# Transposing the meta queries' probabilities from full tiles of 128 rows

## The chip, the cores and the metric

One core of a Trainium2 chip runs the whole network in one launch. The metric is device time in microseconds (us); the kernel before is given by the median of three runs, and one further execution was profiled.

## The reference

A four-layer encoder works on 272 tokens (16 learned meta tokens and 256 grid tokens) of 2048 features in float32. Each layer projects its input into queries, keys, values and a gate, attends, multiplies by the SiLU of the gate, projects back, adds the residual times a constant and normalises:

```python
proj = h @ w_in                       # q, k, v, z
y    = attention(q, k, v) * silu(z)   # by layer: A, B, C, A
h    = layer_norm(ALPHA * h + y @ w_out[i])
```

Layer kind A is attention in a window of the grid plus the meta keys, 16 heads; here the 16 meta queries attend to the 16 meta keys alone. Kind B is differential attention, 8 heads of two softmaxes each, a = p1 - lambda * p2, over all 272 keys; here the meta queries attend to all keys without bias. Kind C is a sliding window with a sink in the softmax, 16 heads that share 4 key heads; here the meta queries again attend to the meta keys alone. In the last layer the meta tokens are no longer needed as queries.

## The kernel before

Everything lies with features on the partitions and tokens on the free axis, in the order: 128 grid tokens, 16 meta tokens, 128 grid tokens. A projection of 128 output features is 16 contraction steps of three matmuls each (`mm3`, lines 146 to 150: high times high, high times low, low times high, in a float32 form of 12 significant bits), each with 128x128 weights and 272 moving columns. The weights stream in from HBM, and ScalarE (line 156) and VectorE (line 157) split them into the high and low part.

Around this one long stream of weight matmuls on TensorE (`run`, lines 817 to 878) the rest is done by background tasks, Python generators that are advanced one step for each four contraction steps (`step`, line 183). The attention of a head is such a task: `attn_a`, `attn_b` or `attn_c`. A planner that simulates the timeline then sets the order of the instructions on each engine, from the dependencies and the order in which they were written; so a task's TensorE instructions stand between weight matmuls in the places that the planner gives them. At the borders between layers the norm of the one layer has to be finished on VectorE, ScalarE and GpSimd before the weight matmuls of the next can go on.

In each attention the probabilities P of 128 + 128 grid queries (tile `s`) and 16 meta queries (tile `s2`, 16 partitions) lie with queries on the partitions. For P times V they are transposed by TensorE into one PSUM tile `tr`. A transposition is a float32 matmul whose stationary operand is the data, loaded as weights, and whose moving operand is the identity matrix `ident`: as many columns move as the data has rows.

- Layer A, `attn_a`: lines 453 and 460 transpose four 96-key pieces of the grid queries, line 455 the meta queries: stationary 16 rows x 96 columns, moving 16 columns. Line 463 transposes the values. The tile `s2` is zeroed on GpSimd for each head (line 413), since only columns 32 to 47 are written.
- Layer B, `attn_b`: lines 528, 529 and 530 run twice per head, for the keys 0 to 127 and 144 to 271; line 529 is that of the meta queries (stationary 16x128, moving 16). Lines 534 to 536 transpose the keys 128 to 159, laid side by side three times by `thrice` (line 364, a GpSimd copy at line 372); line 535 is that of the meta queries (16x96, moving 16). Lines 544 and 545 transpose the values.
- Layer C, `attn_c`: line 648 transposes the grid queries, lines 649 to 651 the three-fold keys; line 650 is that of the meta queries (16x96, moving 16). Before it GpSimd zeroes `s2_mid` for each head (line 370) and copies into it (line 372).

So in layers A, B and C there are 16, 8 x 2 + 8 and 16 transpositions with 16 rows, 56 in all; the last layer has none. The setup (line 231 on) makes `ident`, the constants and the input operands; GpSimd's queue there also issues small loads, such as `lnp` (line 261), the norms' parameters, which ScalarE splits along with the first weights.

Of the kernel before, what the change touches and what calls it, by code (L numbers as in the profile page):

```python
# [11 lines left out]
F32 = mybir.dt.float32  # L12
# [8 lines left out]
META = 16  # L21
NTOK = SEQ + META
# [5 lines left out]
ALPHA = (2 * DEPTH) ** 0.25  # L28
# [3 lines left out]
CHUNK = 4  # L32
LOOKAHEAD = 8
WARM = 8
DEFERRED = 7  # column tiles of a layer that multiply u, while its statistics and its input are made
TAIL = (8, 10, 11)  # first k of the last norm whose subtraction and product GpSimd does, and whose affine VectorE
SETS = (("hh", "hl"), ("yh", "yl"))
BUFS = {"raw": 3, "wh": LOOKAHEAD + 1, "wl": LOOKAHEAD + 1, "qh": 2, "ql": 2, "kh": 2, "kl": 2,
        "vs": 2, "ez": 1, "gate": 3, "bias": 2, "s": 3, "s2": 2, "nm": 4, "sm": 4, "nm2": 4, "sm2": 4,
# [4 lines left out]
# Token order on chip: grid columns 0..31 (row index fastest), the meta tokens,  # L44
# grid columns 32..63.  Tiles keep it as [2, 144]; the last 16 columns are unused.
# [8 lines left out]
def in_tiles(kind):  # L54
    """Column tiles of an input projection in the order of their use: (key, tile)."""
    t = []
    if kind == "A":
        for h in range(16):
            t += [(("q", h), h), (("k", h), 16 + h), (("v", h), 32 + h), (("z", h), 48 + h)]
    elif kind == "B":  # L60
        for h in range(8):
            t += [(("q", 2 * h), 2 * h), (("k", 2 * h), 16 + 2 * h),
                  (("q", 2 * h + 1), 2 * h + 1), (("k", 2 * h + 1), 16 + 2 * h + 1),
                  (("v", 2 * h), 32 + 2 * h), (("v", 2 * h + 1), 32 + 2 * h + 1),
                  (("z", 2 * h), 48 + 2 * h), (("z", 2 * h + 1), 48 + 2 * h + 1)]
    else:
        for g in range(4):
            h = 4 * g
            t += [(("k", g), 16 + g), (("v", g), 20 + g)]
            order = [("q", h), ("q", h + 1), ("z", h), ("q", h + 2), ("z", h + 1),  # L70
                     ("q", h + 3), ("z", h + 2), ("z", h + 3)]
            t += [((n, i), i if n == "q" else 24 + i) for n, i in order]
    return t


def granules(layer):
    """(matrix, column tile, first k, key) in the order in which TensorE takes them."""
    out = []
    t = in_tiles(KINDS[layer])
    if layer == 0:  # L80
        for k0 in range(0, KT, GRAN):
            out += [("in", e, k0, key) for key, e in t[:3]]
        t = t[3:]
    else:
        for key, e in t[:2]:
            out += [("in", e, k0, key) for k0 in range(0, KT - GRAN, GRAN)]
        out += [("in", e, KT - GRAN, key) for key, e in t[:2]]
        t = t[2:]
    for key, e in t:
        out += [("in", e, k0, key) for k0 in range(0, KT, GRAN)]  # L90
    for m in range(3):
        out += [("out", m, k0, ("o", m)) for k0 in range(0, KT - GRAN, GRAN)]
    out += [("out", m, KT - GRAN, ("o", m)) for m in range(3)]
    for m in range(3, KT):
        out += [("out", m, k0, ("o", m)) for k0 in range(0, KT, GRAN)]
    return out
# [18 lines left out]
class Emit:  # L115
# [36 lines left out]
    def hilo(self, src, hi, lo, scale=None):  # L152
        """hi + lo == scale * src, hi with 12 significant bits."""
        nc = self.nc
        if scale is None:
            nc.scalar.copy(out=hi, in_=src)  # L156
            nc.vector.tensor_sub(out=lo, in0=src, in1=hi.bitcast(F32))  # L157
        else:
            nc.scalar.activation(hi, src, AF.Copy, scale=scale)
            nc.vector.scalar_tensor_tensor(out=lo, in0=src, scalar=scale, in1=hi.bitcast(F32),  # L160
                                           op0=ALU.mult, op1=ALU.subtract)

    def column_sums(self, src, view):
        """The sums over the 128 features, on every partition."""
        nc = self.nc
        h, l = self.tok(F32R, "sumh"), self.tok(F32R, "suml")
        self.hilo(view(src), view(h), view(l))
        yield
        p = self.ptok("sc")
        nc.tensor.matmul(view(p), lhsT=self.ones_r, rhs=view(h), start=True, stop=False)  # L170
        nc.tensor.matmul(view(p), lhsT=self.ones_r, rhs=view(l), start=False, stop=True)
        return p

# [57 lines left out]
    def setup(self, nlayers):  # L231
        nc = self.nc
# [9 lines left out]
        x = [self.tok(F32, f"yh{k}") for k in range(KT)]  # L242
# [16 lines left out]
        nc.gpsimd.memset(self.zero, 0.0)  # L259
        self.lnp = self.st([128, DEPTH, KT, 2], F32, "lnp")  # L260
# [14 lines left out]
    def lam_task(self):  # L275
        """-lambda of the differential attention on every partition."""
# [17 lines left out]
    def rows(self, key, acc, view, l, scale=None):  # L294
        """(x, b) with the projection of the layer's input = x + b, and each times scale.

        The first tiles of a layer but the first multiply u = g * d, g and b of the norm before them:
        W' h = (W' u - mean * W' g) * rstd + W' b.  The other tiles multiply h itself."""
# [34 lines left out]
    def evac_gate(self, key, acc, view, l):  # L333
        """z * sigmoid(z)"""
# [11 lines left out]
    def finish(self, k, y, view):  # L346
        """y of 128 features into the operands of the output projection."""
# [8 lines left out]
    def stack(self, src, tag, low):  # L356
        """Rows 0..95 of src hold one block three times: hi, but lo in the 32 rows from low."""
# [5 lines left out]

    def thrice(self, tag, src):
        """src [p, ..., n <= 32] as [p, ..., 3, 32], the rest 0."""
# [38 lines left out]
    def attn_a(self, h, last):  # L404
        """Window attention: query tile 0 sees the key columns 0..191, tile 1 the columns 96..271."""
# [5 lines left out]
        if not last:  # L411
            s2 = self.st([META, 96], F32, "s2")
            nc.gpsimd.memset(s2, 0.0)
# [17 lines left out]
        if not last:  # L431
            p2, nm2, sm2 = s2[:, 32:48], self.st([META, 1], F32, "nm2"), self.st([META, 1], F32, "sm2")
# [14 lines left out]
        # The chunks of P: 0 of tile 0, then 1 of tile 0, the meta queries and 0 of tile 1, for the keys 96..191  # L447
        # that these share, then 1 of tile 1.
# [3 lines left out]
        for c in range(3):  # L452
            nc.tensor.transpose(tr[:96, at[c]:at[c] + 128], s[:, c // 2, c % 2 * 96:c % 2 * 96 + 96], ident)  # L453
        if not last:
            nc.tensor.transpose(tr[:96, 256:272], s2, ident[:META, :META])
# [26 lines left out]
    def attn_b(self, h):  # L482
# [5 lines left out]
        for j in range(2):  # L488
# [3 lines left out]
            s2 = self.st([META, NTOK], F32, "s2")  # L492
# [19 lines left out]
            e.append((s, s2))  # L512
            sums.append((sm, sm2))
# [10 lines left out]
        s_mid, s2_mid = self.thrice("s_mid", s[:, :, mid]), self.thrice("s2_mid", s2[:, mid])  # L524
        ph, pl = self.st([128, 2, NTOK], F32R, "ph"), self.st([128, 2, NTOK], F32R, "pl")
        for c, ks in enumerate(keys):
            tr = self.pt("tr")
            nc.tensor.transpose(tr[:, 0:128], s[:, 0, ks], ident)
            nc.tensor.transpose(tr[:, 128:144], s2[:, ks], ident[:META, :META])
# [5 lines left out]
        nc.tensor.transpose(tr[:96, 128:144], s2_mid, ident[:META, :META])  # L535
# [43 lines left out]
    def rsqrt(self, src, scale, view=None):  # L579
        """(src * scale + 1e-5) ** -0.5 with one Newton step."""  # L580
# [23 lines left out]
    def attn_c(self, h):  # L604
# [5 lines left out]
        s2 = self.st([META, META + 1], F32, "s2")  # L610
# [33 lines left out]
        s_mid, s2_mid = self.thrice("s_mid", s[:, :, 128:160]), self.thrice("s2_mid", s2[:, :META])  # L644
# [5 lines left out]
        nc.tensor.transpose(tr2[:96, 128:144], s2_mid, ident[:META, :META])  # L650
# [21 lines left out]
    def residual(self, l, m, view):  # L672
        """ALPHA * h of 128 features, less the pivot where that is known in time."""
# [12 lines left out]
    def on_out(self, l, m, acc, view, last):  # L686
        """d = residual sum less a pivot (the mean of the first 512 features); its sums, and g * d as operands."""
# [55 lines left out]
    def norm_stats(self, l, view, last):  # L743
        """-mean of d, and the reciprocal of the deviation, of each token on every partition."""
# [29 lines left out]
    def normalise(self, l):  # L774
        """The input of layer l itself, from u."""
# [41 lines left out]
    def run(self, nlayers):  # L817
# [4 lines left out]
        for l in range(nlayers):  # L822
# [12 lines left out]
            if l:  # L835
                self.tasks.append(self.normalise(l))
            for which, e, k0, key in granules(l):
# [48 lines left out]
def weight_chunks(mats, nlayers):  # L886
    """The granules of all matrices, in the order of their use, CHUNK to a row of 8 KB per partition."""
# [8 lines left out]
def window_bias(rpb):  # L896
    """rpb laid out per head as [query, keys of tile 0, keys of tile 1]; 0 at the meta keys, -1e30 outside."""
# [58 lines left out]
```

## Time and profile before

| | |
|---|---|
| median of three runs | 2023.39 us (2023.30 to 2023.46) |
| span of the profiled execution, the only time that it gives | 2021.7 us, 1.7 below that median |
| TensorE, matmuls | 1975.4 us busy, 98% |
| TensorE, weight loads (beside the matmuls) | 1957.0 us, 97% |
| VectorE | 1456.9 us, 72% |
| ScalarE | 1107.3 us, 55% |
| GpSimd | 676.2 us, 33% |
| HBM | 159 GB/s over the span |

The share of the span says which engine is occupied, but a matmul's recorded duration runs on while the next has begun, so that what a matmul costs is read from the distance of its start to the next one's start, which is called its pitch below. Idle time of an engine that is not the bottleneck costs nothing.

### The profile page before, as it was taken

Reading aid. Unit: us, or ns where it says so; the run is one execution under the profiler, and the core shown is the slowest. Engines: PE = TensorE matmul, PEld = TensorE weight load, DVE = VectorE, ACT = ScalarE, POOL = GpSimd, SP = SyncE. Lnnn points to the kernel's source line nnn. Section 1 sums busy time; section 2 is a strip of 40 time slices with the busy share of each in tenths; the row PEclk is TensorE's granted clock in tenths of the full one; section 3 lists DMA queues with packets and bytes.
Section 4 is the critical chain, followed back from the end, with each engine's and each line's share of the span. In section 5 each row is a group of like instructions: output and inputs, shape, how many; then the busy total and the mean of one; then the engine's idle time right before and its main releaser. Section 6 shows DMA issues by size and latency. Waiting matters only on the chain.

```text
span 2021.7 us, 40776 instructions
## 1 busy us (share of the span) xinstructions
PE 1975.4 (98%) x15794; PEld 1957.0 (97%) x15794; DVE 1456.9 (72%) x2617; ACT 1107.3 (55%) x2396; POOL 676.2 (33%) x975
## 2 busy tenths in 40 slices
PE   9999999999989999999999899999998999999995
PEld 9999999999989999999999899999998999999995
DVE  7666666667998677777779986766898666666665
ACT  6555555455655555555556555655555555555553
POOL 2110011118683122212396832323965111111075
PEclk9999999999999999999999999999999999999998
DMA  8444444444534444444445244344444444554442
GB/s 289 156 160 169 160 169 160 165 152 162 189 125 147 148 166 147 159 160 148 148 165 188 105 156 158 139 157 158 161 171 149 166 169 170 175 174 162 162 166 84
DMA packets 52466, 324.00 MB, mean 160 GB/s; under 512 B 5904, under 2 KB 12064, under 8 KB 14768
## 3 DMA queue, kind: packets, MB, share of 16 engines
q1 hardware_dynamic: 51984, 320.76, 44.9%
q8 instruction: 124, 2.03, 0.4%
q0 software_dynamic: 288, 0.63, 0.1%
q14 instruction: 70, 0.57, 0.1%
HBM read 319.27 MB, written 2.10 MB: 159 GB/s over the span
## 4 chain that ended last, share of the span: by engine, by line
PE 92%; DVE 5%; issue 1%; POOL 1%; DMA 0%; ACT 0%; SPq 0%; DVEq 0%; POOLq 0%
PE acc L150 28%; PE acc L148 28%; PE acc L149 28%; DVE wl L157 2%; PE sc L150 1%; PE sc L149 1%; PE sc L148 1%; PE o L150 1%; PE o L149 1%; DVE ht L783 1%; PE o L148 1%; PE tr L453 1%; PE tr L463 1%; DVE yl L788 0%; DVE hl L788 0%
## 5 line engine op out<-in xcount | busy, mean ns | idle before, releaser
L157 DVE TENSOR_TENSOR wl<-raw,wh 128x512 fp32r<-128x512 f32 x1184 | 904.5, 770 | 458.7 <-ACT wh L156 446.5
L156 ACT CAST wh<-raw 128x512 fp32r<-128x512 f32 x1184 | 723.1, 618 | 629.7 <-PE acc L149 602.9
L150 PE MATMUL acc<-yh,wl 128*128 128x272 f32 (+2 forms) x2448 | 708.7, 289 | 0.0
L148 PE MATMUL acc<-yh,wh 128*128 128x272 f32 (+2 forms) x2448 | 706.3, 289 | 0.0
L149 PE MATMUL acc<-yl,wh 128*128 128x272 f32 (+2 forms) x2448 | 703.2, 287 | 0.0
L148 PE MATMUL acc<-hh,wh 128*128 128x272 f32 (+3 forms) x2288 | 660.9, 289 | 6.4 <-ACT wh L156 6.4
L149 PE MATMUL acc<-hl,wh 128*128 128x272 f32 (+3 forms) x2288 | 663.6, 290 | 0.0
L150 PE MATMUL acc<-hh,wl 128*128 128x272 f32 (+3 forms) x2288 | 661.6, 289 | 0.2 <-DVE wl L157 0.2
L149 PEld LDWEIGHTS acc<-yl,wh 128*128 128x128 f32 x2448 | 463.0, 189 | 0.1
L148 PEld LDWEIGHTS acc<-yh,wh 128*128 128x128 f32 x2448 | 461.9, 189 | 0.3
L150 PEld LDWEIGHTS acc<-yh,wl 128*128 128x128 f32 x2448 | 462.0, 189 | 0.0
L148 PEld LDWEIGHTS acc<-hh,wh 128*128 128x128 f32 x2288 | 433.1, 189 | 7.3 <-ACT wh L156 7.1
L150 PEld LDWEIGHTS acc<-hh,wl 128*128 128x128 f32 x2288 | 433.2, 189 | 0.8 <-DVE wl L157 0.7
L149 PEld LDWEIGHTS acc<-hl,wh 128*128 128x128 f32 x2288 | 432.9, 189 | 0.5
L342 DVE RECIPROCAL ez<-ez 128x272 f32<-128x272 f32 (+1 forms) x64 | 116.7, 1824 | 22.7 <-POOL ez L340 22.7
L410 POOL MEMSET s<- 128x16 f32 x32 | 3.6, 112 | 354.2 <-PE tr L460 351.9
L343 POOL TENSOR_TENSOR gate<-gate,ez 128x272 f32<-128x272 f32 (+1 forms) x64 | 66.0, 1031 | 104.1 <-DVE ez L342 99.9
L340 POOL TENSOR_SCALAR ez<-ez 128x272 f32<-128x272 f32 (+1 forms) x64 | 27.2, 425 | 205.4 <-ACT ez L339 205.3
L739 POOL TENSOR_TENSOR os<-os,sq 128x272 f32<-128x272 f32 (+1 forms) x59 | 62.9, 1066 | 0.0
L784 POOL TENSOR_TENSOR ht<-ht,rstd 128x272 f32<-128x272 f32 x48 | 50.4, 1061 | 26.2 <-DVE rstd L769 15.8
L738 POOL TENSOR_TENSOR os<-os,r 128x272 f32<-128x272 f32 x45 | 47.8, 1063 | 19.7 <-DVE r L691 19.7
L680 ACT ACTIVATE ht<-ht 128x272 f32<-128x272 f32 (+1 forms) x64 | 27.2, 426 | 45.6 <-POOL ht L678 45.4
(257 smaller groups left out, 2067.8 us busy)
## 6 DMA issues: line engine op xcount, KB each, us to landing
raw<-in_wts SPq DMA_DIRECT2D x293, 1024.0 KB, 4.8
bias<-in_bias_a SPq DMA_DIRECT2D x32, 184.0 KB, 2.3
raw<-in_wts SPq DMA_DIRECT2D x12, 256.0 KB, 5.6
yh<-in_xT SPq DMA_DIRECT2D x16, 136.0 KB, 4.9
out_h<-raw SPq DMA_DIRECT2D x8, 256.0 KB, 2.1
dist<-in_dist_b POOLq DMA_DIRECT2D x1, 272.0 KB, 6.3
dist<-in_dist_c POOLq DMA_DIRECT2D x1, 272.0 KB, 4.8
lnp<-in_lnp POOLq DMA_DIRECT2D x1, 64.0 KB, 4.2
```

The lines of the kernel that those rows point to most:

```text
L148: mm(out, lhsT=lh, rhs=rh, start=start, stop=False)
L149: mm(out, lhsT=lh, rhs=rl, start=False, stop=False)
L150: mm(out, lhsT=ll, rhs=rh, start=False, stop=stop)
L156: nc.scalar.copy(out=hi, in_=src)
L157: nc.vector.tensor_sub(out=lo, in0=src, in1=hi.bitcast(F32))
L340: nc.gpsimd.tensor_scalar(out=view(ez), in0=view(ez), scalar1=1.0, scalar2=1.0, op0=ALU.mult, op1=ALU.add)
L342: nc.vector.reciprocal(view(ez), view(ez))
L343: nc.gpsimd.tensor_tensor(out=view(zc), in0=view(zc), in1=view(ez), op=ALU.mult)
L680: nc.scalar.activation(h, h, AF.Copy, scale=ALPHA)
L738: nc.gpsimd.tensor_tensor(out=view(self.s1), in0=view(self.s1), in1=d, op=ALU.add)
L739: nc.gpsimd.tensor_tensor(out=view(self.s2), in0=view(self.s2), in1=sq, op=ALU.add)
L784: nc.gpsimd.tensor_tensor(out=t, in0=t, in1=whole(rstd), op=ALU.mult)
```

## The change

The meta queries' probabilities get tiles of 128 partitions whose rows 16 to 127 are zeroed once, in the setup, on GpSimd: two tiles of 128x272 that the heads take in turn (`meta_tile`), and one of 128x96 for the three-fold keys (`meta_mid`). The softmax still works on the first 16 rows. The transposition takes all 128 rows as stationary operand and all 128 columns of the identity as moving operand; it writes 128 columns of PSUM where 16 are wanted, and the transposition that follows overwrites the other 112. In layer A the meta queries' transposition therefore moves ahead of that of the last 96-key piece of the grid queries. The zeroing per head in layers A (line 413) and C (line 370) is gone; at the start of layer C the 16 rows of `meta_mid` are zeroed once. `first` in layer B is the whole tile of which `s2` of the first softmax is the first 16 rows.

```diff
 setup:
+        self.meta = [self.st([128, NTOK], F32, f"s2{i}") for i in "ab"]
+        self.meta_mid = self.st([128, 3, 32], F32, "s2_mid")
+        for t in self.meta + [self.meta_mid]:
+            nc.gpsimd.memset(t, 0.0)
 new:
+    def meta_tile(self):
+        self.meta.reverse()
+        return self.meta[0]
 attn_a:
-            s2 = self.st([META, 96], F32, "s2")
-            nc.gpsimd.memset(s2, 0.0)
+            s2 = self.meta_tile()
...
-            p2, nm2, sm2 = s2[:, 32:48], ...
+            p2, nm2, sm2 = s2[:META, 32:48], ...
...
         for c in range(3):
+            if c == 2 and not last:
+                nc.tensor.transpose(tr[:96, 256:384], s2[:, :96], ident)
             nc.tensor.transpose(tr[:96, at[c]:at[c] + 128], s[:, c // 2, c % 2 * 96:c % 2 * 96 + 96], ident)
-        if not last:
-            nc.tensor.transpose(tr[:96, 256:272], s2, ident[:META, :META])
 attn_b:
-            s2 = self.st([META, NTOK], F32, "s2")
+            t2 = self.meta_tile()
+            s2 = t2[:META]
...
+            first = t2 if j == 0 else first
...
-        s_mid, s2_mid = self.thrice("s_mid", s[:, :, mid]), self.thrice("s2_mid", s2[:, mid])
+        s_mid = self.thrice("s_mid", s[:, :, mid])
+        nc.gpsimd.tensor_copy(out=self.meta_mid[:META], in_=s2[:, mid].unsqueeze(1).to_broadcast([META, 3, 32]))
+        s2_mid = self.meta_mid.rearrange("p a b -> p (a b)")
...
-            nc.tensor.transpose(tr[:, 128:144], s2[:, ks], ident[:META, :META])
+            nc.tensor.transpose(tr[:, 128:256], first[:, ks], ident)
...
-        nc.tensor.transpose(tr[:96, 128:144], s2_mid, ident[:META, :META])
+        nc.tensor.transpose(tr[:96, 128:256], s2_mid, ident)
 attn_c:
-        s2 = self.st([META, META + 1], F32, "s2")
+        s2 = self.meta_tile()[:META, :META + 1]
...
-        s_mid, s2_mid = self.thrice("s_mid", s[:, :, 128:160]), self.thrice("s2_mid", s2[:, :META])
+        s_mid = self.thrice("s_mid", s[:, :, 128:160])
+        nc.gpsimd.tensor_copy(out=self.meta_mid[:META, :, :META], in_=s2[:, :META].unsqueeze(1).to_broadcast([META, 3, META]))
+        s2_mid = self.meta_mid.rearrange("p a b -> p (a b)")
...
-        nc.tensor.transpose(tr2[:96, 128:144], s2_mid, ident[:META, :META])
+        nc.tensor.transpose(tr2[:96, 128:256], s2_mid, ident)
 run:
+            if l and kind == "C":
+                nc.gpsimd.memset(self.meta_mid[:META], 0.0)
```

## Rows read from the trace of the kernel before

**Rows 1.** Busy us (count) by stretch: PE, PEld, DVE, ACT, POOL; clock, DMA share, GB/s.
```profile
30.00:540.00 510.00, 510.00 (x4109) 507.14 (x4109) 336.98 (x617) 268.92 (x578) 118.15 (x185) 1.00 0.48 167
...
612.00:1100.00 488.00, 487.97 (x3867) 482.75 (x3866) 363.62 (x662) 279.86 (x622) 158.32 (x227) 1.00 0.45 159
1100.00:1160.00 60.00, 53.79 (x392) 51.13 (x391) 59.77 (x106) 35.72 (x85) 51.11 (x65) 0.94 0.33 119
1160.00:1500.00 340.00, 340.00 (x2733) 337.17 (x2732) 259.19 (x482) 195.40 (x430) 146.19 (x243) 1.00 0.44 157
```

**Rows 2.** TensorE's groups with 16 rows: form, count, busy us, modelled mean ns, idle before.
```profile
L529 PE MATMUL tr<-ident,s 16*128 16x16 f32 x16 | 3.7, 230 | 1.3 <-DVE s L521 1.3
L650 PE MATMUL tr<-ident,s_mid 16*96 16x16 f32 x16 | 3.5, 217 | 0.0
L455 PE MATMUL tr<-ident,s 16*96 16x16 f32 x16 | 3.5, 216 | 0.0
L535 PE MATMUL tr<-ident,s_mid 16*96 16x16 f32 x8 | 1.7, 215 | 0.0
```

**Rows 3.** Timeline of TensorE, layer A, last head: start us, duration us, engine, line, form.
```profile
436.62 0.29 PE L148 MATMUL acc<-hh,wh 128*128 128x272 f32 x1
436.84 0.22 PE L455 MATMUL tr<-ident,s 16*96 16x16 f32 x1
436.99 0.39 PE L149 MATMUL acc<-hl,wh 128*128 128x272 f32 x1
437.22 0.29 PE L150 MATMUL acc<-hh,wl 128*128 128x272 f32 x1
...
437.60 0.29 PE L150 MATMUL acc<-hh,wl 128*128 128x272 f32 x1
```

**Rows 4.** Timeline of TensorE, last layer, one head: seven transpositions between two weight matmuls.
```profile
1903.10 0.28 PE L148 MATMUL acc<-yh,wh 128*128 128x256 f32 x1
1903.22 0.49 PE L453 MATMUL tr<-ident,s 128*96 128x128 f32 x3
...
1904.10 0.28 PE L150 MATMUL acc<-yh,wl 128*128 128x256 f32 x1
```

**Rows 5.** Timeline of TensorE, layer B, the two key halves of one head.
```profile
698.55 0.29 PE L148 MATMUL acc<-yh,wh 128*128 128x272 f32 x1
...
699.64 0.28 PE L150 MATMUL acc<-yh,wl 128*128 128x272 f32 x1
```

**Rows 6.** Timeline of TensorE, layer B, the keys 128 to 159 of one head.
```profile
812.91 0.28 PE L149 MATMUL acc<-yl,wh 128*128 128x272 f32 x1
...
813.99 0.29 PE L148 MATMUL acc<-yh,wh 128*128 128x272 f32 x1
```

**Rows 7.** Timeline of TensorE, layer C, one head.
```profile
1222.25 0.28 PE L150 MATMUL acc<-hh,wl 128*128 128x272 f32 x1
...
1222.89 0.29 PE L149 MATMUL acc<-hl,wh 128*128 128x272 f32 x1
```

**Rows 8.** Timeline of TensorE, layer C: matmuls of 128 rows with 16 moving columns.
```profile
1199.49 0.17 PE L148 MATMUL sc<-kh,qh 128*16 128x16 f32 x1
1199.52 0.17 PE L149 MATMUL sc<-kl,qh 128*16 128x16 f32 x1
```

**Rows 9.** Line 455 alone: the waits of TensorE's queue (count, ns, first to last start).
```profile
L455 PEldq EVENT_SEMAPHORE  x14: 51/51/51, 37.4 to 434.6; - x14
```

**Rows 10.** Timeline of VectorE, layer A, last head: scaling of the meta probabilities.
```profile
434.06 0.21 DVE L445 TENSOR_SCALAR s<-s,sm 16x16 f32<-16x16 f32 x1
```

**Rows 11.** Timeline of GpSimd at the start.
```profile
0.74 0.20 POOL masks.py:197 MEMSET ident<- 128x128 f32 x1 [0.29 <-POOLq L945]
1.30 0.74 POOL L261 DMA_DIRECT2D lnp<-in_lnp  x1 [0.32 <-issue]
```

**Rows 12.** Timeline of ScalarE at the start.
```profile
5.81 0.29 ACT L156 CAST lnh<-lnp 128x128 fp32r<-128x128 f32 x1
...
9.15 0.62 ACT L156 CAST wh<-raw 128x512 fp32r<-128x512 f32 x1 [1.12 <-DMA raw<-in_wts]
```

More of the change, by code (lines that the diff above doesn't have):

```diff
@@ L38 @@
 BUFS = {"raw": 3, "wh": LOOKAHEAD + 1, "wl": LOOKAHEAD + 1, "qh": 2, "ql": 2, "kh": 2, "kl": 2,
-        "vs": 2, "ez": 1, "gate": 3, "bias": 2, "s": 3, "s2": 2, "nm": 4, "sm": 4, "nm2": 4, "sm2": 4,
+        "vs": 2, "ez": 1, "gate": 3, "bias": 2, "s": 3, "nm": 4, "sm": 4, "nm2": 4, "sm2": 4,
         "ph": 1, "pl": 1, "pm": 1, "vm": 2, "ht": 5, "r": 4, "gb": 2, "vh": 2, "vl": 2,
@@ L431, in attn_a @@
         if not last:
-            p2, nm2, sm2 = s2[:, 32:48], self.st([META, 1], F32, "nm2"), self.st([META, 1], F32, "sm2")
+            p2, nm2, sm2 = s2[:META, 32:48], self.st([META, 1], F32, "nm2"), self.st([META, 1], F32, "sm2")
             nc.vector.tensor_tensor_reduce(out=p2, in0=sc[:META, part[2]], in1=self.zero,
```

## The prediction

> **What bounds the kernel now.** I read the page's shares first, then the engines' busy time by stretch, then TensorE's timeline at each kind of place that the change touches. In the stretches that hold the bulk of layers A, B and C, TensorE is busy all the time: 510.00 of 510 us, 487.97 of 488 and 340.00 of 340, while VectorE, the next, has 66%, 75% and 76% [rows 1]. There a nanosecond of TensorE is a nanosecond of the kernel. At the border before layer C it is the other way round: VectorE has 59.77 of 60 us and TensorE 53.79 [rows 1]; what TensorE saves before its last wait there is worth nothing.
>
> A matmul's recorded duration overlaps with the next, so I go by pitch, from start to start. A weight matmul of 272 columns costs 0.127: from 437.22 to 437.60 three of them start [rows 3]. A transposition with 128 rows and 128 moving columns costs 0.109: in the last layer's head a weight matmul starts at 1903.10 and the second one after it at 1904.10; between them stand seven transpositions (three on line 453, one on 460, three on 463) and one weight matmul [rows 4]. The two weight matmuls, of 256 columns there, take 0.12 each (1903.10 to 1903.22), which leaves 0.76 for seven. This sum holds the change from one kind of matmul to the other as well.
>
> **The change, part by part.** *The transpositions of the meta queries.* There are 16 (line 455), 16 (line 529), 8 (line 535) and 16 (line 650), 56 with 16 rows [rows 2]. The groups give 216 to 230 ns of modelled duration to each, and no idle time to speak of, so this view hides what they cost. The pitch shows it:
>
> Layer A: from the weight matmul at 436.62 to the second one after it, at 437.22, are 0.60 us: two weight matmuls (2 x 0.127) and line 455 in between [rows 3]. So line 455 costs 0.35, of which only 0.15 lies behind its own start (436.84 to 436.99); 0.09 is the matmul before it, which takes 0.22 until line 455 may start, and 0.10 the one behind it (436.99 to 437.22). The same pattern stands at 15 of the 16 heads. With 128 rows it should cost 0.109: 0.24 less. In the first head it stands between full transpositions and costs what line 535 does, below. 15 x 0.237 + 0.17 = 3.7 us.
>
> Layer B, key halves: 698.55 to 699.64 are 1.09 us with two weight matmuls, two of line 529 and two of line 530, which alternate [rows 5]. 1.09 - 0.25 - 4 x 0.109 = 0.40 too much for a pair, and 8 pairs make 3.2 us. All eight look alike; the 1.3 us that one of them waits for VectorE [rows 2] stand ahead of it, so that its pauses, behind that wait, count too.
>
> Layer B, keys 128 to 159: 812.91 to 813.99 are 1.08 us with two weight matmuls, five full transpositions and line 535 [rows 6]. 1.08 - 0.25 - 6 x 0.109 = 0.17; 8 heads make 1.4 us.
>
> Layer C: 1222.25 to 1222.89 are 0.64 us with two weight matmuls, line 650 and line 651 [rows 7]. 0.64 - 0.25 - 2 x 0.109 = 0.17; 16 heads make 2.8 us, less 0.2 for the first one, which I place before TensorE's last waits at the border (the stretch to 1160 [rows 1]): 2.6.
>
> Sum: 3.7 + 3.2 + 1.4 + 2.6 = 10.9 us. What the trace does not show is the new shape itself, 128 rows of which 112 are zero. From below it can cost 0.027, the pitch of the matmuls with 128 rows and 16 columns (1199.49 to 1199.52) [rows 8]; I exclude that, since 128 columns move, and take 0.109 from the full transpositions [rows 4], which have the same rows and columns. From above it costs as much as now (0.28 to 0.35) plus the added columns, which is the second rival.
>
> Why the 16 rows should be to blame: matmuls with 16 columns but 128 rows pass at 0.027 without a pause around them [rows 8], and a full transposition of float32 data at 0.109 [rows 4]; neither few columns nor the data's type makes the pause. Only the forms with 16 rows have it, all four of them. The Trainium skill, "TensorEngine Tiling (Array Packing)", section Key Properties, says that a change of the tiling mode drains TensorE; a pause ahead of the 16-row matmul and another behind it are what that would look like, though no row names the mode. Against it speaks the same skill's "TensorE: Matmul & The Clock Gate", section Step-by-step: what each phase is for, by which the load of weights goes with the columns and the row count does not matter, and one moving column enters in a cycle. By that page the change has nothing to win from rows and pays for 112 columns more, an estimate of 47 ns at 2.4 GHz or 2.6 us in all; it is the second rival's rule.
>
> *The moved order in layer A.* The meta queries' transposition now stands ahead of the last 96-key piece, so that this one too waits for the scaling on line 445. That ends at 434.27 [rows 10], and the wait of TensorE's queue for line 455 is over at 434.6 [rows 9], 2.2 us before line 455 runs at 436.84 [rows 3]: the queue is that far ahead of the array. I put it at nothing. If that cover went, the weight matmuls behind would wait too, at worst one VectorE operation of 0.2 per head [rows 10], 3 us over 16.
>
> *GpSimd.* The zeroing per head goes, 16 times 0.17 in A and as often in C; no engine on the path waits for it, so it is worth nothing. In the setup three memsets come before the load of `lnp` (issued at 1.30 [rows 11]). One of 128x128 has 0.20 [rows 11]; from that 128x272 is some 0.35 (an estimate, by columns), so that the load goes out 0.5 to 0.9 later. Behind it waits ScalarE's split of `lnp` at 5.81, and behind that the casts of the input. But ScalarE stands idle for 1.12 us before 9.15, for a weight load on SP's queue, which nothing here moves [rows 12], so at most a few tenths reach the first matmuls and are made up there: between 0 and 0.3, I take 0. Layer C's one memset lies on GpSimd at the border, and there, too, I take 0.
>
> *What is late next.* PSUM evictions have the same width as before, and VectorE at 75% to 76% has room for a TensorE that is 1% faster in B and C [rows 1]. The borders between layers are a chain from the last output projection through the norm; they move forward with TensorE as they are.
>
> **Time.** The profiled execution spans 2021.7 us, 1.7 below the median of 2023.39; I subtract from the median. 2023.4 - 10.9 = 2012.5 us.
>
> **Rivals.** First, the planner's new order gives part of it back. It plans with more columns for 56 matmuls, and so may put other work elsewhere; near the borders, where VectorE is full (59.77 of 60 [rows 1]), a changed order can lengthen TensorE's waits. If B and C lose what they won and A's 3.7 stays, the time is 2019.7; if A's is lost as well, 2023. For it: 53.79 of 60 at that border shows that order matters there. Against it: all but one of the places counted lie in stretches without a wait.
>
> Second, slower: the pause is not of the 16 rows but of the place, the queue's wait (14 of the 16 of line 455 have one of their own [rows 9]) or a weight load that isn't taken ahead, and stays; then only the columns count. From 16 to 128 moving columns the pitch goes from 0.027 to 0.109 [rows 4, 8], 0.082 x 56 = 4.6, and the time is 2028.0. Over the 0.027 of a short matmul the pauses sum to 15.5 (10.9 + 4.6), of which 4.6 must go for no change: the rival decides where more than 70% of them stay. Against it: lines 535 and 650 have no wait of their own in the queue and the same pause.
>
> Third, it does nothing: the pauses go, but the zeroed tiles add dependencies between heads (a tile is overwritten while the transposition two heads back still reads it). But layer A's 16 heads [rows 2] share a stretch of 510 us [rows 1], so that the transposition two heads back is long done; 2021 to 2024.
>
> **How the numbers follow.** Forecast 0.78, at 2012.5, with its own range from 2010 to 2015 (each pitch read to 0.01 over 56 places gives 0.6; the rest is order). The first rival 0.10, half of it at 2019 or less; the second 0.06; the third 0.06. A measurement of this kernel can tell 0.2%, 4 us, from no change, so faster means below 2019.3: 0.78 + 0.05 = 0.83; slower, above 2027.4: 0.06 and a little of the others, 0.07; the rest, 0.10, is no change. The range leaves out the second and third rival and the worse half of the first: 2009 to 2019.
>
> **What would show it.** Right: TensorE's timeline shows the meta transpositions with 128 rows at a pitch of about 0.11, the matmul before them at its usual 0.127; TensorE's sum in 30 to 540 holds the same work in 3.7 us less; the borders are as long as before. Wrong: a pitch of 0.2 or more before or behind the new transpositions (second rival), or waits of TensorE inside the bulk stretches, or longer borders (first).

## The result and the profile after

The changed kernel takes 2008.18 us (median of four runs, 2007.29 to 2008.72) against 2023.43 for the one before; the ratio is 0.9921, 95% interval 0.9910 to 0.9933. It is faster by 15.2 us where 10.9 were forecast, and lies 0.8 us below the low end of the range, 2009.0.

The page of the changed kernel, its span and engines:

```profile
span 2005.5 us, 40741 instructions
...
PE 1957.6 (98%) x15794; PEld 1948.7 (97%) x15794; DVE 1456.4 (73%) x2617; ACT 1105.0 (55%) x2396; POOL 677.1 (34%) x947
```

The span fell by 16.2 us, from 2021.7, with the same number of matmuls and, to one point, the same shares. TensorE's timeline of the changed kernel at the four kinds of place that the prediction priced (lines 463, 542, 548 and 665 are the meta queries'):

```profile
435.00 0.29 PE L149 MATMUL acc<-hl,wh 128*128 128x272 f32 x1
435.13 0.27 PE L463 MATMUL tr<-ident,s2a 128*96 128x128 f32 x1
435.24 0.27 PE L464 MATMUL tr<-ident,s 128*96 128x128 f32 x1
435.26 0.37 PE L150 MATMUL acc<-hh,wl 128*128 128x272 f32 x1
435.47 0.29 PE L148 MATMUL acc<-hh,wh 128*128 128x272 f32 x1
...
693.76 0.29 PE L148 MATMUL acc<-yh,wh 128*128 128x272 f32 x1
693.89 0.27 PE L542 MATMUL tr<-ident,s2b 128*128 128x128 f32 x1
...
694.45 0.28 PE L150 MATMUL acc<-yh,wl 128*128 128x272 f32 x1
...
805.58 0.29 PE L148 MATMUL acc<-yh,wh 128*128 128x272 f32 x1
...
805.81 0.27 PE L548 MATMUL tr<-ident,s_mid 128*96 128x128 f32 x1
...
806.48 0.29 PE L150 MATMUL acc<-yh,wl 128*128 128x272 f32 x1
...
1211.27 0.29 PE L150 MATMUL acc<-hh,wl 128*128 128x272 f32 x1
1211.39 0.27 PE L665 MATMUL tr<-ident,s_mid 128*96 128x128 f32 x1
...
1211.74 0.29 PE L149 MATMUL acc<-hl,wh 128*128 128x272 f32 x1
```

The pauses are gone. In layer A two weight matmuls and two transpositions take 0.47 (435.00 to 435.47), which is 2 x 0.126 and 2 x 0.109; the matmul ahead of line 463 keeps its 0.13, where it had 0.22 ahead of line 455 [rows 3]. In layer B's key halves 0.69 stand in place of 1.09 [rows 5], in its keys 128 to 159 0.90 in place of 1.08 [rows 6], in layer C 0.47 in place of 0.64 [rows 7]. Those are the prices of the prediction to 0.01.

So the surplus is elsewhere, and the last layer shows where: it has no meta queries. The start of the first transpositions of two of its heads, six heads apart, in the kernel before:

```profile
1747.54 0.49 PE L453 MATMUL tr<-ident,s 128*96 128x128 f32 x3
```

(the other one is the second row of [rows 4], at 1903.22), and in the changed kernel:

```profile
1732.24 0.49 PE L464 MATMUL tr<-ident,s 128*96 128x128 f32 x3
...
1886.42 0.49 PE L464 MATMUL tr<-ident,s 128*96 128x128 f32 x3
```

Six heads take 155.68 before and 154.18 now, 0.25 us a head less, with the same instructions in the same order on TensorE. It is not the clock: the granted clock, third from the right, is 1.00 in both, before and after:

```profile
1620.00:1900.00 280.00, 280.00 (x2311) 280.00 (x2310) 174.53 (x312) 145.65 (x301) 28.27 (x50) 1.00 0.48 168
```

```profile
1620.00:1900.00 280.00, 280.00 (x2335) 280.00 (x2335) 176.69 (x316) 147.50 (x306) 28.39 (x50) 1.00 0.49 171
```

The groups of the weight matmuls that the operands yh and yl feed (busy us, modelled mean ns), before:

```profile
L150 PE MATMUL acc<-yh,wl 128*128 128x272 f32 x1872 | 543.9, 291 | 0.0
L148 PE MATMUL acc<-yh,wh 128*128 128x272 f32 x1872 | 541.7, 289 | 0.0
L149 PE MATMUL acc<-yl,wh 128*128 128x272 f32 x1872 | 537.6, 287 | 0.0
```

and after:

```profile
L148 PE MATMUL acc<-yh,wh 128*128 128x272 f32 x1872 | 538.4, 288 | 0.0
L149 PE MATMUL acc<-yl,wh 128*128 128x272 f32 x1872 | 537.6, 287 | 0.0
L150 PE MATMUL acc<-yh,wl 128*128 128x272 f32 x1872 | 537.2, 287 | 0.0
```

Even the modelled duration of an unchanged weight matmul fell, on line 150 by 4 ns. By pitch the 5370 or so of them that stand among their like (steps of up to 150 ns) went from 125.9 to 124.4 ns on the mean, while those that hh and hl feed stayed at 125.1 to 125.3. With all starts of the two traces sorted by what stands there, the 16.1 us between the first and the last matmul come out like this (us, before and after, worked out from every pair of neighbouring starts; "like for like" allows for matmuls that the new order puts into another row):

```
transpositions and their neighbours     100.15 ->  91.75   (17 more matmuls count as neighbours: -10.5 like for like)
weight matmuls fed by yh, yl            885.37 -> 874.40   -11.0
weight matmuls fed by hh, hl            827.71 -> 828.85   +1.1 (12 fewer: +2.6 like for like)
steps of over 262 ns (waits)             38.46 ->  40.78   +2.3
everything else                         147.47 -> 147.24   -0.2
```

What differs for yl is its place. The programs' SBUF addresses show it: the new tiles are made in the setup, ahead of everything that is allocated later, so yl and most of the attention's tiles lie 384 or 2560 bytes higher. The weights' parts wh and wl, and yh, hh and hl, lie where they lay. yl now starts 163456 bytes behind yh, before it was 163072; hl has always been 1152 behind hh. That holds for 15 of the 16 contraction steps: five other tiles lie ahead of the last step's yl, so that it is 5760 bytes further from its yh, before and after.

### The profile page after: what moved, and what is told of

Read it like the earlier page. It is cut to its first block, busy times and chain, and to the rows that moved or that the text cites. A ratio compares the mean times of both kernels' runs of the same rounds, so it can differ in the third digit from the quotient of the medians.

```text
span 2005.5 us, 40741 instructions
## 1 busy us (share of the span) xinstructions
PE 1957.6 (98%) x15794; PEld 1948.7 (97%) x15794; DVE 1456.4 (73%) x2617; ACT 1105.0 (55%) x2396; POOL 677.1 (34%) x947
## 4 chain that ended last, share of the span: by engine, by line
PE 93%; DVE 5%; issue 1%; POOL 1%; DMA 0%; ACT 0%; SPq 0%; DVEq 0%; POOLq 0%
PE acc L148 28%; PE acc L150 28%; PE acc L149 28%; DVE wl L157 1%; PE sc L150 1%; PE sc L148 1%; PE sc L149 1%; PE o L150 1%; PE o L149 1%; DVE ht L798 1%; PE o L148 1%; PE tr L464 1%; PE tr L472 1%; DVE yl L803 0%; DVE yl L822 0%
## 5 line engine op out<-in xcount | busy, mean ns | idle before, releaser
L150 PE MATMUL acc<-yh,wl 128*128 128x272 f32 (+2 forms) x2448 | 700.7, 286 | 0.0
```

The lines of the kernel that those rows point to most:

```text
L150: mm(out, lhsT=ll, rhs=rh, start=False, stop=stop)
```

## The experiments

Two theories: P, some 10 us are the shape of the transpositions and the rest is the tiles' places; S, the shape explains it all. And for the cause of the pause: the rows, or the moving columns.

**Old shape, new places.** The kernel before, with its two tags set aside in the setup:

```diff
         nc.gpsimd.memset(self.zero, 0.0)
+        for shape, tag in (([META, NTOK], "s2"), ([META, NTOK], "s2"), ([META, 3, 32], "s2_mid")):
+            nc.gpsimd.memset(self.st(shape, F32, tag), 0.0)
```

> The kernel before, with 16-row transpositions, but its tiles s2 and s2_mid are set aside early in the setup, so that every tile has the SBUF address that it has in the changed kernel (yl 384 bytes higher, wh, wl, yh, hh and hl where they were). Theory P (shape and placement): the change's 15.2 us are some 10.9 from the shape of the transpositions and the rest from the places of the tiles, seen as a shorter pitch of the weight matmuls fed by yh and yl (mean 125.9 to 124.4 ns). Then this kernel is 3 to 9 us faster than before, 2014 to 2020, and its yh and yl matmuls have the pitch of the changed kernel. Theory S (shape alone: the pauses cost more than the pitch showed): places do nothing, 2022.5 to 2024.5, pitch as before.

Measured: 2018.10 against 2023.68, ratio 0.9973 (0.9963 to 0.9983), 5.6 us faster with every 16-row transposition still there; pitch of the yh and yl matmuls 124.5. P holds, S does not.

**New shape, old places.** The changed kernel with the tiles made at their first use:

```diff
-        self.meta = [...]; self.meta_mid = ...; memsets     # in the setup
+        if not self.meta:                                    # in meta_tile, and the like for meta_mid in attn_b
+            self.meta = [self.st([128, NTOK], F32, f"s2{i}") for i in "ab"]
+            for t in self.meta:
+                self.nc.gpsimd.memset(t, 0.0)
```

> The changed kernel, but its meta tiles are made when the first head needs them, so that every tile lies at the SBUF address of the kernel before. Theory P: the gain is the shape's alone, 9 to 12 us off the kernel before, 2011.5 to 2014.5 (the prediction's 2012.5), and the yh and yl matmuls have the pitch of before. Theory S: 2007 to 2009.5, like the changed kernel.

Measured: 2013.87, ratio 0.9952 (0.9939 to 0.9964), 9.8 faster; pitch 125.9. The same two heads of the last layer, in this kernel:

```profile
1738.90 0.49 PE L465 MATMUL tr<-ident,s 128*96 128x128 f32 x3
...
1894.58 0.49 PE L465 MATMUL tr<-ident,s 128*96 128x128 f32 x3
```

155.68, to the hundredth what the kernel before has. Compared at the same weight matmuls of line 148, this trace wins on that of the kernel before 3.7 us between 33.5 and 439.6 us (layer A's attention; times of the kernel before), 4.6 in layer B and 2.7 in layer C, and in between and behind nothing, to 0.1: the terms of the prediction are 3.7, 3.2 + 1.4 and 2.6. It had lost 2.3 us in the first 33.5. The two halves, 5.6 and 9.8, add up to the whole, 15.2, within what the intervals allow.

**80 and 64 rows.** Both with the new places:

```diff
-  nc.tensor.transpose(tr[:96, 256:384], s2[:, :96], ident)
+  nc.tensor.transpose(tr[:96, 256:256+n], s2[:n, :96], ident[:n, :n])    # n = 80 or 64; the other three alike
```

> The changed kernel with 80 rows and 80 moving columns in the meta queries' transpositions instead of 128 (the program gives them the full array). If the pause belongs to forms of few rows that the program places on a part of the array, there is none here, and the cost is between that of the changed kernel and 2.3 us less (0.109 x 48/128 x 56): 2005.5 to 2008.7. If the cost goes with the moving columns alone, it falls on from here to 64 rows.

> The same with 64 rows and 64 moving columns; the program gives them half of the array's rows. If a form that takes a part of the array's rows makes the pause, it is back: 8 to 15 us more than with 80 rows, 2014 to 2021. If the cost goes with the moving columns, 0.7 us less than with 80 rows, 2005 to 2008.

Measured: 80 rows 2006.07, ratio 0.9912 (0.9899 to 0.9926); 64 rows 2019.34, ratio 0.9976 (0.9967 to 0.9985), 13.3 us slower than 80 though fewer columns move. The last head of layer A with 80 rows:

```profile
433.77 0.29 PE L149 MATMUL acc<-hl,wh 128*128 128x272 f32 x1
433.90 0.23 PE L463 MATMUL tr<-ident,s2a 80*96 80x80 f32 x1
433.97 0.27 PE L464 MATMUL tr<-ident,s 128*96 128x128 f32 x1
434.00 0.37 PE L150 MATMUL acc<-hh,wl 128*128 128x272 f32 x1
434.20 0.28 PE L148 MATMUL acc<-hh,wh 128*128 128x272 f32 x1
```

and with 64:

```profile
437.09 0.29 PE L149 MATMUL acc<-hl,wh 128*128 128x272 f32 x1
437.31 0.26 PE L463 MATMUL tr<-ident,s2a 64*96 64x64 f32 x1
437.50 0.32 PE L464 MATMUL tr<-ident,s 128*96 128x128 f32 x1
437.57 0.37 PE L150 MATMUL acc<-hh,wl 128*128 128x272 f32 x1
437.78 0.28 PE L148 MATMUL acc<-hh,wh 128*128 128x272 f32 x1
```

With 80 rows the five starts span 0.43 (0.47 with 128: fewer columns do cost less, 0.07 in place of 0.11), with 64 they span 0.69, and the pause is back on both sides: 0.22 ahead and 0.19 behind. The step lies between 64 and 80 rows. The programs as built place the matmuls of 16 rows on 32 rows of the array, those of 64 on 64, and those of 80 and 128 on all 128. The Trainium skill, "TensorEngine Tiling (Array Packing)", section Available Configurations, names tiles of 32, 64 and 128 rows, and its section Key Properties says that a change of the tiling mode drains TensorE; these rows agree, with 0.22 ahead and 0.19 behind for 64 rows where 80 have 0.13 and 0.07. The Trainium skill, "TensorE: Matmul & The Clock Gate", section Step-by-step: what each phase is for, says of the load of weights that the row count does not matter; as a rule for the whole transposition, the use that the second rival made of it, that fails here (0.69 against 0.43).

**Which tile's place.** First the new shape at the old places, with 384 bytes left free ahead of yl alone (in `finish`, at its first use):

```diff
+        if (self.layer, k) == (0, 0):
+            nc.gpsimd.memset(self.st([128, 96], F32, "pad"), 0.0)
```

> The run with the new shape and the old places, with 384 bytes left free just before yl, so that yl (and what lies behind it: ht, r, os and others) has the address that it has in the changed kernel, while the attention's tiles ahead of it stay at the old places. Theory Y (the distance of yl from the other operands of the weight matmuls sets their pitch): yh and yl matmuls of 272 columns at 124.4 to 124.7 ns, 2007 to 2010 us. Theory Q (the tiles of the attention ahead of yl, moved by 2560 or 384 bytes, matter): pitch stays at 125.9, 2012.5 to 2015.

Measured: 2004.73, ratio 0.9906 (0.9889 to 0.9922), pitch 124.4. So it is yl's place, theory Y. The run is even 3.5 us faster than the changed kernel: the other tiles seem to have been better off where they were.

Then the 80-row kernel with 128, 256 and 384 bytes in the same spot:

> The 80-row kernel (2006.1 us) with yl moved up by 128 bytes. yl lies 163072 bytes behind yh in the kernel before (256 over a multiple of 512), 163456 in the changed one (128 over, as hl behind hh); here 163584 (256 over). Theory M (what counts is that distance modulo 512): pitch back at 125.9, 2010 to 2013. Theory of another period: anything else, 2004 to 2014 by its pitch.

> The same with 256 bytes: the distance is 163712, 384 over a multiple of 512. Theory M: another pitch than at 128 and 256 over, or one of them; 2004 to 2013. If the pitch does not depend on the distance at all: 2005 to 2007 here and with 128 and 384 bytes.

> The same with 384 bytes: the distance is 163840, a multiple of 512. Theory M: if both operands lying alike is what collides, the slowest of the four, 2010 to 2018; if it helps, the fastest, 2000 to 2005. No dependence: 2005 to 2007.

Measured: 2012.92, 2005.28 and 2012.97, ratios 0.9948 (0.9933 to 0.9963), 0.9908 (0.9893 to 0.9923) and 0.9947 (0.9932 to 0.9962), beside 2006.07 with none; pitches 125.9, 124.7, 125.9 and 124.7. Theory M had the wrong period: slow at 256 and at 0 over a multiple of 512, fast at 128 and 384, so it is the distance modulo 256 that tells them apart. The two heads with 128 bytes:

```profile
1736.22 0.49 PE L466 MATMUL tr<-ident,s 128*96 128x128 f32 x3
...
1892.29 0.49 PE L466 MATMUL tr<-ident,s 128*96 128x128 f32 x3
```

156.07, where the kernel before has 155.68: 128 bytes of unused memory cost 6.9 us. That is put to the test from the other side, on the kernel before with nothing else changed, 128 bytes ahead of yl:

> The kernel before with nothing changed but 128 bytes left free ahead of yl, so that yl lies an odd multiple of 128 bytes behind yh (163200) instead of a multiple of 256 (163072). Theory D (that distance modulo 256 sets the pitch of the weight matmuls fed by yh and yl): their pitch falls from 125.9 to 124.4 to 124.7 ns, 6700 matmuls or so by 1.3 to 1.5, 2013 to 2017 us. Theory A (what counted were the moves by 256 to 384 bytes in the runs so far, or other tiles): pitch 125.9, 2022 to 2025.

Measured: 2014.97 against 2023.72, ratio 0.9954 (0.9939 to 0.9969), 8.7 us; pitch 124.6. The two heads:

```profile
1740.56 0.49 PE L455 MATMUL tr<-ident,s 128*96 128x128 f32 x3
...
1895.16 0.49 PE L455 MATMUL tr<-ident,s 128*96 128x128 f32 x3
```

154.60. As theory D has it: at 439.6 us, where the first matmuls fed by yh and yl start, the two traces are 0.04 us apart, and at 537.5, behind layer A's output projection, 1.8. The three remaining runs:

> 80 rows, tiles at the old places but yl 128 bytes up (distance 163200, odd multiple of 128). With the new places the same 128 bytes cost 7 us; theory D says that here they gain as much: pitch 124.4 to 124.7, 2001 to 2006, the fastest of all. If the address of yl itself counted and not the distance, 2009 to 2014.

Measured: 2001.34 (2001.10 to 2001.89), ratio 0.9886 (0.9872 to 0.9901), pitch 124.7: faster than both kernels, by 22.4 and 6.8 us. The expectation's second answer does not test what it names: yh stands still in all these runs, so that a rule on yl's own place modulo 256 would give the same as one on the distance.

> The 80-row kernel at the new places with yl 64 bytes up: distance 163520, 192 over a multiple of 256. Theory D in steps of 128 bytes: fast or slow as a neighbour, 2005 to 2007 or 2012 to 2014. If it goes gradually: in between, 2008 to 2011.

Measured: 2006.02, ratio 0.9910 (0.9895 to 0.9925), pitch 124.9: 192 over behaves like 128 over in the time and nearly so in the pitch, where a course in proportion would give 125.3.

> The 80-row kernel with wl 128 bytes up, and yl 256 bytes up so that its distance from yh stays an odd multiple of 128. wl is the low part of the weights, and lay a multiple of 256 behind wh. If the distance between weights counts as well, the pitch of all weight matmuls changes by 1 ns or more, 13 us or more either way. If only the moving operands' distance counts: 2004 to 2007, pitches 124.4 to 124.7 and 125.1.

Measured: 2009.60, ratio 0.9927 (0.9910 to 0.9943). Neither answer: the yh and yl matmuls stay at 124.7 with 272 columns, the hh and hl matmuls go from 125.1 to 125.6, and those of yh and yl with 256 columns from 117.9 to 119.2. Against the run with 256 bytes, whose yl lies in the same place, it is 4.3 us slower. The weights' places may have an effect of their own, much smaller than the 13 us that were named; the run moved hh4 to hh15 and most of the attention's tiles by 128 bytes too, so it doesn't say which.

## Why the prediction was wrong

The time was outside the range because a term was missing from the sum; the terms that stood in it were right.

- *Transpositions, 10.9 us.* Right in place and size: the trace gives 10.5 like for like, and the run with the shape alone 9.8, with 3.7, 4.6 and 2.7 in the places that were named. That the 16 rows were to blame, and not the place, the queue's wait or the columns (the second rival), is shown by 64 against 80 rows.
- *The short matmuls, 0.027 without a pause around them.* Misread, without harm to the forecast. In the trace of the kernel before, the weight matmul behind three of them takes 0.21 in place of 0.127:

```profile
1199.54 0.17 PE L150 MATMUL sc<-kh,ql 128*16 128x16 f32 x1
1199.57 0.37 PE L149 MATMUL acc<-hl,wh 128*128 128x272 f32 x1
1199.78 0.29 PE L150 MATMUL acc<-hh,wl 128*128 128x272 f32 x1
```

  From 1199.49 [rows 8] to 1199.78 are 0.29; less 0.127, that is 0.054 for each. The second rival would then have been (0.109 - 0.054) x 56 = 3.1 us slower, at 2026.5 and not 2028.0; 0.054 is still far from the 0.28 to 0.35 with 16 rows.
- *"What is late next" and the sum's silence on everything untouched.* This step failed. The sum took every instruction that the change does not name at its old cost, and the range left nothing below 2009 for it. But the change also moves where tiles are made, the allocator then puts yl 384 bytes higher, and some 7070 weight matmuls that the diff does not touch take 11.0 us less. Before, yl lay a multiple of 256 bytes behind yh, and now it lies an odd multiple of 128 behind it, in all but the last contraction step. Nothing in the profile of before names an address; what its starts did show, and I did not read, is that weight matmuls of one shape had a pitch of 125.9 ns fed by yh and yl and 125.1 fed by hh and hl.
- *The rest gives some back.* Moving the other tiles costs about 3: the old shape gains 8.7 with yl alone moved and 5.6 with all of them moved, the new shape 3.5 more with the others left in place. Part of it is seen (the hh and hl matmuls of 256 columns have 118.4 to 118.5 ns with the attention's tiles at the old places and 119.3 at the new ones, though 117.8 there with 64 bytes ahead of yl; TensorE's waits sum to 2.3 us more), the cause of it stays open. Of the 2.9 us between the traces of the two old-shape runs, 2.0 stand in the first 75 us, ahead of the first use of yl; at that point the traces of the other kernels lie anywhere from 0.5 us ahead of that of the kernel before to 2.0 behind it, so single traces do not share it out.
- *The moved order in layer A, at nothing.* Right: line 463 starts 0.13 behind the weight matmul ahead of it, without a wait.
- *GpSimd in the setup, at nothing.* Right for the load and its split; for the kernel it is not shown. The timeline of GpSimd in the changed kernel:

```profile
1.19 0.33 POOL L263 MEMSET s2b<- 128x272 f32 x1
...
1.92 0.75 POOL L265 DMA_DIRECT2D lnp<-in_lnp  x1
```

  and that of ScalarE:

```profile
6.40 0.29 ACT L156 CAST lnh<-lnp 128x128 fp32r<-128x128 f32 x1
...
9.38 0.62 ACT L156 CAST wh<-raw 128x512 fp32r<-128x512 f32 x1 [1.50 <-DMA raw<-in_wts]
```

  0.33 for a memset estimated at 0.35, and the load of `lnp` 0.6 later than at 1.30 [rows 11]; the split of it stands further back, at 6.40 in place of 5.81 [rows 12], and ScalarE still waits 1.50 us for the weights of 9.38, in place of 9.15. TensorE runs behind at the start: the ninth weight matmul of line 148, at 11.05 us before, is 1.55 later in the changed kernel, and the 161st, at 74.61 before, 0.50. At the 161st the runs with the memsets in the setup lie from 0.5 ahead of the kernel before to 2.0 behind it, those without from 0.3 ahead to 1.7 behind, so no run shows what the setup costs by itself.
- *First rival, the planner's order.* It changed, as feared, most of all around the border to layer C. TensorE's longer waits, 2.3 us in all, are at most a tenth or so of what was won (10.5 + 11.0). The third rival, that nothing comes of it, fell with the first measurement.

## What to carry to other kernels

Price a small matmul by the starts around it, from the matmul ahead of it to the second one behind, not by its duration: 16 rows among 128-row matmuls cost 0.17 to 0.24 us more than a zero-padded full one, and 80 rows were enough to avoid it. A change that makes, drops or moves a tile moves the addresses of all that are allocated after it, and a kernel bound by TensorE can feel that: before crediting a change with its whole gain, run it with the old addresses, and the old kernel with the new ones. Where two operand tiles alternate as moving operand and lie a multiple of 256 bytes apart, try the second one 128 bytes further; here that alone was worth 8.7 us.

## What was not expected of the hardware

Weight matmuls with 272 moving columns take their moving operand in turn from yh, yl and yh. Their mean pitch is 125.9 ns with yl a multiple of 256 bytes behind yh (the distances 163072, that of the kernel before, 163584 and 163840) and 124.4 to 124.9 otherwise (163200, 163456, 163520, 163712). Shown by the runs is that yl's place decides, since it alone, with what lies behind it, is moved by 128 bytes; yh was never moved.

That the distance between the two operands counts, and not yl's own place, is argued from the contraction steps. The triple of lines 148, 149 and 150 takes 377.1 ns for even and 378.2 for odd steps in the kernel before, and 372.5 and 373.5 in the changed one (without the last step). The addresses of yh and yl advance by 1152 bytes a step, an odd multiple of 128, so that a place of yl relative to something that stands still would show in every second step alone.

Two things speak against a rule as simple as that. In the last step, where yl lies 5760 bytes further, the distance is a multiple of 256 in the changed kernel and an odd multiple of 128 in the kernel before. In the changed kernel the step takes 376.5 ns, slow among its like, as the rule would have it; in the kernel before it takes 378.4 and is no faster than the other odd steps. And the size of the gain depends on more: in layer A's output projection, where the kernel before has 125.8 ns, the runs with yl off a multiple of 256 have 123.5 if their meta transpositions have 16 or 128 rows, but 124.4 to 125.0 if they have 64 or 80. Which part of the memory or of the engine is contended for, no run here shows.
